# The first half of a mixing product as one block of 1024 columns, three of its eight pairs in seven products instead of eight

## The chip, the cores and the metric

The kernel runs on one core of a Trainium2 chip. Its engines work side by side, each through its own list of instructions in order: TensorE (PE: matmuls, and PEld, the loads of their stationary operand), VectorE (DVE), ScalarE (ACT), GpSimd (POOL) and SyncE (SP, which here only issues DMAs). The metric is the device time of one execution in microseconds; lower is better.

## The reference, cut to what matters

One decoder layer on 256 tokens of 2048 features in float32: a half feed-forward, two token mixers side by side (retention and windowed attention), a second half feed-forward, and a gated embedding, each followed by a layer norm. The change touches the product that joins the two mixers:

```python
mixed = (jax.nn.sigmoid(gate_r) * ret_branch + jax.nn.sigmoid(gate_a) * att_branch) @ w_mix_out[i]
h = layer_norm(alpha * h + mixed, ln_g[i, 1], ln_b[i, 1])
```

The matrix `w_mix_out` is 2048 x 2048.

## The kernel before, in words

**Float32 by three matmuls.** Every float32 operand is split into a high part of a format that PE takes at full speed and a low part, which is the rest (`split`, L97 to L99: ACT writes the high part, then DVE subtracts it from the value to get the low one). One product of 128 x 128 by 128 x 512 then is three matmuls: low by high, high by high, high by low (`Sum.add`, L367 to L376). The order is that: the low part of the tokens' operand is the first thing that PE reads.

**The mixing product before.** Tokens are in two halves t of 128. The 2048 features that are summed over come in 16 groups k of 128, two groups to a *pair* p (0 to 7). The 2048 output columns are made in four blocks of 512 (`mo0` to `mo3`), with one PSUM bank per block and token half; there are eight banks. `tokens_out` (L386) goes through the eight chunks of one block; a chunk is the weights of one pair for 512 columns (128 x 1024 numbers, 512 KB) and costs 2 groups x 2 halves x 3 = 12 matmuls. The residual `y[blk]` is loaded from DRAM when the block starts; after the block DVE adds 1.19 times it (L1474) and takes the statistics of the layer norm (`block_stats`, L744). The fourth block goes through another routine with the norm.

**The features.** The product's left operand is made just before it. The retention block `mr1` ends with DVE forming two arrays of 512 features, `sig[2]` and `sig[3]` (L1454, L1455). PE turns them (transposes, 128 x 128 at a time; `turned`, L1428 to L1436), two groups at a time, and ACT and DVE split the turned values into `mix_t[p]`. Pairs 0 to 3 were turned during `mr1`; pairs 4 to 7 are turned while the first mixing block already runs. These turns are *side jobs*: a list `side`, of which `run_side` (L310) takes one after every chunk or unit of the matmuls. One idle job stands ahead of the four turns. `run_side` also advances `lazy`, which here makes operands for the second feed-forward ahead of time and stores them to DRAM (`sums_ahead`, L219: two DVE sums, a few side steps later two more, then two low parts, and stores on SP's queue).

**Sevens.** In other parts of the kernel (feed-forwards, gates, `mr0` and `mr1`) a block of 1024 columns takes some pairs as *sevens*: a product of 2 x 2 blocks (two token halves, two groups of features; two groups of features, two column halves) with seven block products in place of eight, so 21 matmuls for 24 (`block`, L404). A seven needs more of DVE. Its weights (`Seven.make`, L160) take four sums of weight blocks and four low parts, where the two plain chunks that it replaces take two low parts. On the side of the features it needs four combinations `f5`, `f6`, `f7`, `f3` of the quarters of two groups (`seven_forms`, L438; with `whole`, which puts high and low back together, and a split of the result: `forms_of`, L460, makes those of two pairs at once). Steps go to four extra banks `p1`, `p6`, `p7`, `q5` and to three of the four result banks; after the last seven DVE and ACT combine the extra ones (`seven_common`, L476, the *fold*). In a seven that is not the last, the order of steps is p1 (no form), q2 (no form), q3 (form `f3`), q5, p7, p6, q4; in the last one it is p1, q5 (form `f5`), p6, p7, q2, q3, q4. The retention blocks have sevens for pairs 0 and 1, and their forms (`mrf`) are made well ahead, during the attention's product.

**What sets the order of the work.** All instructions are emitted in a fixed order; an engine never takes a later one first. A planner (`fill`, L260) emits loads and preparations ahead of use. It counts time in matmuls (12 for a plain chunk, 21 for a seven) and space in slots of 128 x 1024 numbers. It prepares the next loaded item while less than 45 of matmul time is ready and the item's `makes` fit (2 slots for a plain chunk, 6 for a seven, which then keeps 7), and loads the next planned one while ready and loaded together stay below 90. `slots_for_weights(16)` sets its room for the mixing product. It is called in `done`, that is, after the matmuls of each chunk or seven have been emitted and before `run_side`. A tile is bound to its place when it is first written; an engine that gets there early waits for the last reader of what was there.

Of the kernel before, what the change touches and what calls it, by code (L numbers as in the profile page):

```python
# [12 lines left out]
ALU = mybir.AluOpType  # L13
PSUM = bass.MemoryType.PSUM

P = 128
S = 256
# [5 lines left out]
ALPHA = 2.0**0.25  # L23
LN_EPS = 1e-5
GN_EPS = 1e-5
KD = D // P
# [29 lines left out]
def layer(ctx: ExitStack, tc: tile.TileContext, io):  # L56
    nc = tc.nc
    sync, act, dve, pool, pe = nc.sync, nc.scalar, nc.vector, nc.gpsimd, nc.tensor
# [8 lines left out]
    def bank(name):  # L67
        return psum.tile([P, 512], F32, tag="ps", name=name)

    def banks(name):  # L70
        return [bank(name + str(j)) for j in range(2)]
# [217 lines left out]
    def take(key):  # L289
        if not ready:  # L290
            fill(True)
        u = ready.pop(0)
        assert u.key == key, (u.key, key)
        return u

    def done(u):
        room["used"] -= u.keeps
        fill()
# [7 lines left out]
    side = []  # L306
    lazy = []
    idle = lambda: None

    def run_side(n=1):  # L310
        for _ in range(n):
            if side:
                side.pop(0)()
        if lazy and next(lazy[0], "end") == "end":
            lazy.pop(0)
# [65 lines left out]
    def tokens_chunk(chunk, k0, lhs, sums, ts, kks=(0, 1)):  # L381
        for kk in kks:
            for t in ts:
                sums[t].add(half_of(lhs(k0 + kk), t), chunk.columns(kk))

    def tokens_out(key, n_k, lhs, ps, n=512, before=None):  # L386

        nk = 1024 // n
        sums = [Sum(ps[t][:, :n], n_k) for t in range(2)]
        for c in range(n_k // nk):  # L390
            u = take(key + (c,))
            tokens_chunk(u.chunk, c * nk, lhs, sums, (0, 1), range(nk))
            done(u)
            run_side()

    def block_units(units, keys):

        for kind, p in units:
            if kind == "P":
                plan.extend(Single(keys(n, p)) for n in range(2))  # L400
            else:
                plan.append((Seven if kind == "S" else Prepared)(keys(0, p), keys(1, p)))

    def block(name, units, keys, lhs, forms, sums, fold, before=None):  # L404


        sevens = [p for kind, p in units if kind != "P"]
        if sevens:
            p1, p6, p7, q5 = (Sum(bank(f"{name}s{j}"), len(sevens)) for j in range(4))
        for j, (kind, p) in enumerate(units):  # L410
            if before is not None:
                before(j)
            if kind == "P":
                for n in range(2):
                    u = take(keys(n, p))
                    tokens_chunk(u.chunk, 2 * p, lhs, [sums[t][n] for t in range(2)], (0, 1))
                    done(u)
                    run_side()
                continue
            u = take(keys(0, p))  # L420
            a11, a12 = (half_of(lhs(2 * p + e), 0) for e in range(2))
            a22 = half_of(lhs(2 * p + 1), 1)
            f5, f6, f7, f3 = forms(p)
            q2, q3, q4 = sums[0][0], sums[0][1], sums[1][0]
            steps = [
                (p1, a11, u.b11), (q2, a12, u.b21), (q3, f3, u.b22), (q5, f5, u.t1),
                (p7, f7, u.t3), (p6, f6, u.t2), (q4, a22, u.t4),
            ]
            if p == sevens[-1]:
                steps = [steps[j] for j in (0, 3, 5, 4, 1, 2, 6)]  # L430
            for to, left, right in steps:
                to.add(left, right)
            done(u)
            run_side()
            if p == sevens[-1]:
                fold(p1.ap, p6.ap, p7.ap, q5.ap)
# [23 lines left out]
    def forms_of(parts, name):  # L460
        hi, lo = (slot([P, 8, P], F32R, name + w) for w in "hl")
        return seven_forms(whole(parts, name + "w"), hi, lo)
# [8 lines left out]
    def block_sums(ps, units, n_k):  # L471

        s = sum(kind == "S" for kind, p in units)
        return [[Sum(ps[t][n], n_k - (2 * s if t and n else s)) for n in range(2)] for t in range(2)]

    def seven_common(p1, p6, p7, q5):  # L476

        e, w = slot([P, 2, 512], F32, "eve"), slot([P, 2, 512], F32, "evw")
        act.copy(e[:, 0], p1)
        dve.tensor_tensor(w[:, 0], e[:, 0], p6, ALU.add)  # L480
        dve.tensor_tensor(e[:, 1], w[:, 0], p7, ALU.add)
        dve.tensor_tensor(w[:, 0], q5, w[:, 0], ALU.subtract)
        dve.tensor_tensor(w[:, 1], q5, e[:, 1], ALU.subtract)
        return e, w
# [257 lines left out]
    def block_stats(stats, y, col):  # L742
        for t in range(2):
            dve.bn_stats(stats[:, t, col, :], y[col][:, t])  # L744

    def load_columns(src, col, name):
        v = slot([P, 2, 512], F32, f"{name}{col}")
        sync.dma_start(v, src[col])
        return v
# [4 lines left out]
    def load_for_norm(i):  # L754

        vectors.append(ln_vectors(i))
        if i < 2:
            p_raws.append(slot([P, 2, S], F32, "praw"))
            sync.dma_start(p_raws[0], io["pT"])
# [320 lines left out]
    GATE_UNITS = units_of("PPSSPSSP", (0, 1, 2, 3))  # L1080
    RET_UNITS = units_of("PPPSPSPP", (0, 1))
    gate_keys = lambda b: lambda n, p: ("w_in_f2", 29 + 4 * b + 2 * n, p)
    ret_keys = lambda b: lambda n, p: ("w_ret2", 4 * b + 2 * n, p)

    def plan_mixers():
        plan_tokens(("w_rv", 0), KD)
        for grp in range(8):
            plan_features([("w_in_f", grp)], KD)
        for blk in range(1, 4):
            plan_tokens(("w_rv", blk), KD)  # L1090
        for grp in range(8, 16, 2):
            plan_tokens(("w_in_f2", grp), KD)
        plan_tokens(("w_av",), KD, nk=4)
        for grp in (20, 16, 17, 18, 19):
            plan_features([("w_in_f", grp)], KD)
        for grp in range(21, 29, 2):
            plan_tokens(("w_in_f2", grp), KD)
        for b in range(2):
            block_units(GATE_UNITS, gate_keys(b))
        for j in range(0, 8, 2):  # L1100
            plan_tokens(("w_att2", j), KD // 2)
        for b in range(2):
            block_units(RET_UNITS, ret_keys(b))
        for blk in range(4):
            plan_tokens(("w_mix", blk), KD)

    def later(n, job):
# [5 lines left out]
    def mixers(ht, norm, residual, keepers, away):  # L1113
# [18 lines left out]
        ps = banks("rv0")  # L1132
# [16 lines left out]
        for grp in range(8):  # L1149
            ps = banks(f"rqk{grp}")  # L1150
# [6 lines left out]
        for blk in range(1, 4):  # L1157
            ps = banks(f"rv{blk}")
# [99 lines left out]
        for h in range(0, HR, 2):  # L1258
            ps = banks(f"rg{h}")
# [16 lines left out]
        ps = banks("av")  # L1276
# [114 lines left out]
        made = {}  # L1391
        forms = lambda p: made[p // 2](p % 2)
        slots_for_weights(18)
        sig = []
        for j in range(4):
# [5 lines left out]
            ps = banks(f"gt{j}")  # L1401
# [3 lines left out]
                act.copy(sig[-1][:, t], ps[t])  # L1405
        assert not side

        def mixer_block(name, units, keys, lhs):

            ps = [banks(name + w) for w in "ab"]  # L1410
            got = []
            block(name, units, keys, lhs, forms, block_sums(ps, units, KD), lambda *a: got.extend(seven_common(*a)))
            for n in range(2):
                for t in range(2):
                    dve.tensor_tensor(got[n][:, t], got[n][:, t], ps[t][n], ALU.add)
            return got
# [5 lines left out]
        mix_t = []  # L1422
        y = {}
# [15 lines left out]
        for j in range(4):  # L1439
            v = sig[4 + j]  # L1440
# [7 lines left out]
        for b in range(2):  # L1448
            for v in sig[2 * b : 2 * b + 2]:
                act.activation(v, v, AF.Sigmoid)  # L1450
            pr = mixer_block(f"mr{b}", RET_UNITS, ret_keys(b), lambda k: of_pairs(ret_t, k))
            for n in range(2):
                j = 2 * b + n
                dve.tensor_tensor(sig[j], sig[j], pr[n], ALU.mult)  # L1454
                dve.tensor_tensor(sig[j], sig[j], sig[4 + j], ALU.add)  # L1455
            side.append(idle)
            side.extend(lambda v=v, kk=kk: turned(v, kk) for v in sig[2 * b : 2 * b + 2] for kk in (0, 2))

        stats = small.tile([P, 2, 4, 6], F32, tag="stats", name="mixst", bufs=1)
# [4 lines left out]
        lhs = lambda k: of_pairs(mix_t, k)  # L1464
        slots_for_weights(16)
        lazy.append(sums_ahead(ahead[8:], 3, 2))
        for blk in range(3):
            if blk == 2:
                load_for_norm(1)
            ps = banks(f"mo{blk}")  # L1470
            y[blk] = load_columns(residual, blk, "mixy")
            tokens_out(("w_mix", blk), KD, lhs, ps)
            for t in range(2):
                dve.scalar_tensor_tensor(y[blk][:, t], y[blk][:, t], ALPHA, ps[t], ALU.mult, ALU.add)  # L1474
            block_stats(stats, y, blk)
        y[3] = load_columns(residual, 3, "mixy")
        ps = banks("mo3")
        sums = [[Sum(ps[t], KD)] for t in range(2)]
# [316 lines left out]
```

## Time and profile before

| | us |
|---|---|
| median of 3 runs | 2271.42 (2270.95 to 2271.64) |
| span of the profiled execution, first to last instruction | 2269.2 |
| PE busy | 2262.1 |
| DVE busy | 1996.8 |
| ACT busy | 1224.6 |
| first mixing matmul, from the span's start | 1379.63 |
| first matmul of the third mixing block | 1425.06 |

The profile gives the span of its execution; its whole time is not shown apart from that. A row of the order of time reads: start, time taken, engine, line, operation, what it writes and reads, shapes, how many in a row, and in brackets how long the engine stood idle before it and what ended that. A matmul's time taken is its latency: 0.39 us, though a new one starts about every 0.23 us. DVE's and ACT's operations overlap a little at the ends too, so starts are compared rather than durations. A row of waits reads: who waited, for whom, in total, how many times, the longest. In names, numbers of buffers are left out: `mo` is any of the mixing blocks' banks, `mixt` the turned features, `lw_mix` and `hw_mix` the low and high parts of its weights, `uw_`/`vw_` a seven's sums, `mrfh`/`mrfl` the parts of the retention's forms.

### The profile page before, as it was taken

What the parts mean: (1) busy time and instruction counts of PE and PEld (TensorE: products, weight loads), DVE (VectorE), ACT (ScalarE), POOL (GpSimd) and SP (SyncE); (2) the same over time, 40 slices, a digit from 0 to 9 for tenths busy, and PEclk for the clock granted to TensorE, in tenths of its full rate; (3) what the DMA queues carried; (4) which work ended last, traced back from release to release, by engine and by line L of the source; (5) the groups of instructions that cost most, each with busy time, mean ns of one, the idle gap of its engine ahead of it and who ended that gap; (6) DMA issues with size and microseconds to landing.
All of it is one profiled execution on the core that took longest, in us unless ns stands there. A gap on an engine that the chain in (4) does not pass through costs nothing.

```text
span 2269.2 us, 29180 instructions
## 1 busy us (share of the span) xinstructions
PE 2262.1 (100%) x10497; PEld 1880.1 (83%) x10497; DVE 1996.8 (88%) x2586; ACT 1224.6 (54%) x1493; POOL 2.3 (0%) x9
## 2 busy tenths in 40 slices
PE   9999999999999999999999999999999999999998
PEld 8888888888888888888778888888888888888887
DVE  7999999999989887888789788689999999889887
ACT  6555555556555444445566554455555565555543
POOL 0000000000000000000000000000000000000000
PEclk9999999999999999999999999999999999999999
DMA  8666665665587878765446668787867766555872
GB/s 301 206 202 195 197 212 177 205 205 187 211 287 258 293 284 295 255 227 190 145 154 219 194 203 294 278 287 241 299 242 250 257 197 218 197 189 210 290 268 75
DMA packets 211130, 515.72 MB, mean 227 GB/s; under 512 B 16413, under 2 KB 20893, under 8 KB 210985
## 3 DMA queue, kind: packets, MB, share of 16 engines
q1 hardware_dynamic: 209000, 511.28, 66.4%
q10 hardware_dynamic: 1984, 2.58, 0.4%
q8 instruction: 82, 1.34, 0.2%
q14 instruction: 64, 0.52, 0.1%
HBM read 484.43 MB, written 29.36 MB: 226 GB/s over the span
## 4 chain that ended last, share of the span: by engine, by line
PE 99%; DVE 0%; ACT 0%; issue 0%; ACTq 0%; POOL 0%; POOLq 0%
PE f1g L376 3%; PE f1g L374 3%; PE f1g L375 3%; PE f2g L376 3%; PE f2g L374 3%; PE f2g L375 3%; PE rqk L325 3%; PE f1u L376 2%; PE f1u L374 2%; PE f1u L375 2%; PE f2u L374 2%; PE f2u L376 2%; PE f2u L375 2%; PE aqk L325 2%; PE f2d L374 2%; PE f1d L375 2%
## 5 line engine op out<-in xcount | busy, mean ns | idle before, releaser
L99 DVE TENSOR_TENSOR lf_gu<-rf_gu,hf_gu 128x1024 fp32r<-128x1024 f32 (+1 forms) x274 | 323.3, 1211 | 13.1 <-ACT hf_gu L98 12.2
L98 ACT CAST hf_gu<-rf_gu 128x1024 fp32r<-128x1024 f32 (+1 forms) x274 | 274.1, 1043 | 29.9 <-DMA rf_gu<-in_f_gu 29.6
L99 DVE TENSOR_TENSOR lf_down<-rf_down,hf_down 128x1024 fp32r<-128x1024 f32 x150 | 178.8, 1220 | 17.4 <-ACT hf_down L98 15.3
L99 DVE TENSOR_TENSOR lw_in_f<-rw_in_f,hw_in_f 128x1024 fp32r<-128x1024 f32 x140 | 167.5, 1219 | 24.9 <-ACT hw_in_f L98 24.7
L98 ACT CAST hf_down<-rf_down 128x1024 fp32r<-128x1024 f32 x150 | 151.8, 1050 | 48.8 <-DMA rf_down<-in_f_down 22.3
L98 ACT CAST huf_gu<-uf_gu 128x1024 fp32r<-128x1024 f32 x70 | 73.8, 1054 | 146.6 <-DVE uf_gu L171 135.1
L98 ACT CAST hw_in_f<-rw_in_f 128x1024 fp32r<-128x1024 f32 x140 | 140.3, 1050 | 3.0 <-PE rv L375 1.4
L374 PE MATMUL f1g<-hf_gu,xt 128*128 128x512 f32 x247 | 96.5, 391 | 0.0
L376 PE MATMUL f1g<-lf_gu,xt 128*128 128x512 f32 x247 | 96.4, 390 | 0.0
L375 PE MATMUL f1g<-hf_gu,xt 128*128 128x512 f32 x247 | 96.1, 389 | 0.0
L98 ACT CAST hvf_gu<-vf_gu 128x1024 fp32r<-128x1024 f32 x70 | 73.8, 1054 | 29.9 <-DVE vf_gu L173 29.2
L971 ACT ACTIVATE eve<-eve 128x1024 f32<-128x1024 f32 x20 | 21.2, 1062 | 126.1 <-DVE eve L970 126.1
L99 DVE TENSOR_TENSOR luf_gu<-uf_gu,huf_gu 128x1024 fp32r<-128x1024 f32 x70 | 85.3, 1219 | 0.0
L99 DVE TENSOR_TENSOR lvf_gu<-vf_gu,hvf_gu 128x1024 fp32r<-128x1024 f32 x70 | 85.3, 1218 | 0.0
L374 PE MATMUL f2g<-hf_gu,ht 128*128 128x512 f32 x217 | 84.6, 390 | 0.0
L376 PE MATMUL f2g<-lf_gu,ht 128*128 128x512 f32 x217 | 84.5, 390 | 0.0
L375 PE MATMUL f2g<-hf_gu,ht 128*128 128x512 f32 x217 | 84.4, 389 | 0.0
L374 PE MATMUL f1u<-hf_gu,xt 128*128 128x512 f32 x212 | 83.4, 393 | 0.0
L376 PE MATMUL f1u<-lf_gu,xt 128*128 128x512 f32 x212 | 82.5, 389 | 0.0
L375 PE MATMUL f1u<-hf_gu,xt 128*128 128x512 f32 x212 | 82.5, 389 | 0.0
L374 PE MATMUL f2u<-hf_gu,ht 128*128 128x512 f32 x172 | 68.2, 397 | 0.0
L376 PE MATMUL f2u<-lf_gu,ht 128*128 128x512 f32 x172 | 66.9, 389 | 0.0
(1465 smaller groups left out, 6558.1 us busy)
## 6 DMA issues: line engine op xcount, KB each, us to landing
rf_gu<-in_f_gu SPq DMA_DIRECT2D x360, 512.0 KB
rf_down<-in_f_down SPq DMA_DIRECT2D x176, 512.0 KB
rw_in_f<-in_w_in_f SPq DMA_DIRECT2D x148, 512.0 KB
rw_rv<-in_w_rv SPq DMA_DIRECT2D x32, 512.0 KB
rw_ret<-in_w_ret SPq DMA_DIRECT2D x32, 512.0 KB
rw_mix<-in_w_mix SPq DMA_DIRECT2D x32, 512.0 KB
rw_pg<-in_w_pg SPq DMA_DIRECT2D x32, 512.0 KB
rw_att<-in_w_att SPq DMA_DIRECT2D x16, 512.0 KB
```

What stands on the lines that cost most here:

```text
L98: act.copy(dst_hi, src)
L99: (lo_engine or dve).tensor_tensor(dst_lo, src, dst_hi, ALU.subtract)
L325: pe.matmul(ps[f], hi[:, kk, f * P : (f + 1) * P], rhs(k), start=k == 0, stop=k == n_k - 1,)
L374: pe.matmul(o, al, bh, start=first, stop=False)
L375: pe.matmul(o, ah, bh, start=False, stop=False)
L376: pe.matmul(o, ah, bl, start=False, stop=self.left == 0)
L971: act.activation(g, g, AF.Silu)
```

## The change

Blocks 0 and 1 of the mixing product become one block of 1024 columns, `mos`, which goes through `mixer_block` and `block` like the retention blocks. Its units in order are plain pairs 0, 1, 2 (two chunks each, named P0n0, P0n1 and so on by column half), sevens of pairs 4 and 5, plain pair 3, the seven of pair 6, plain pair 7. The sevens thus stand on features that are turned last. Their forms are made in `before_mix`, a function that `block` calls ahead of each unit: those of pairs 4 and 5 right ahead of the seven of pair 4, those of pairs 6 and 7 right ahead of the seven of pair 6, where the residuals of both blocks are loaded as well. The features' turns get two idle jobs ahead of them instead of one, so they come after P1n0, P1n1, P2n0 and P2n1. After the block the residual is added in two operations of 1024 in place of four of 512. Blocks 2 and 3 stay as they were. In `block`, the four extra banks are taken when the first seven is reached, not when the block starts; this holds for every block with sevens.

```diff
         sevens = [p for kind, p in units if kind != "P"]
-        if sevens:
-            p1, p6, p7, q5 = (Sum(bank(f"{name}s{j}"), len(sevens)) for j in range(4))
+        four = []
...
             f5, f6, f7, f3 = forms(p)
+            if not four:
+                four.extend(Sum(bank(f"{name}s{i}"), len(sevens)) for i in range(4))
+            p1, p6, p7, q5 = four
...
+    MIX_UNITS = [("P", 0), ("P", 1), ("P", 2), ("S", 4), ("S", 5), ("P", 3), ("S", 6), ("P", 7)]
+    mix_keys = lambda n, p: ("w_mix", n, p)
...
-        for blk in range(4):
+        block_units(MIX_UNITS, mix_keys)
+        for blk in range(2, 4):
             plan_tokens(("w_mix", blk), KD)
...
-        def mixer_block(name, units, keys, lhs):
+        def mixer_block(name, units, keys, lhs, before=None):
...
-            side.append(idle)
+            side.extend((idle,) * (1 + b))
             side.extend(lambda v=v, kk=kk: turned(v, kk) for v in sig[2 * b : 2 * b + 2] for kk in (0, 2))
...
-        for blk in range(3):
-            if blk == 2:
-                load_for_norm(1)
-            ps = banks(f"mo{blk}")
-            y[blk] = load_columns(residual, blk, "mixy")
-            tokens_out(("w_mix", blk), KD, lhs, ps)
-            for t in range(2):
-                dve.scalar_tensor_tensor(y[blk][:, t], y[blk][:, t], ALPHA, ps[t], ALU.mult, ALU.add)
+        def before_mix(j):
+            if j in (3, 6):
+                made[j // 3 + 1] = forms_of(mix_t[4 + (j == 6) * 2 :][:2], f"mof{j}")
+            if j == 6:
+                for blk in range(2):
+                    y[blk] = load_columns(residual, blk, "mixy")
+
+        for blk, v in enumerate(mixer_block("mos", MIX_UNITS, mix_keys, lhs, before_mix)):
+            dve.scalar_tensor_tensor(y[blk], y[blk], ALPHA, v, ALU.mult, ALU.add)
             block_stats(stats, y, blk)
+        load_for_norm(1)
+        ps = banks("mo2")
+        y[2] = load_columns(residual, 2, "mixy")
+        tokens_out(("w_mix", 2), KD, lhs, ps)
+        for t in range(2):
+            dve.scalar_tensor_tensor(y[2][:, t], y[2][:, t], ALPHA, ps[t], ALU.mult, ALU.add)
+        block_stats(stats, y, 2)
```

More of the change, by code (lines that the diff above doesn't have):

```diff
@@ L1406, in mixers @@
         assert not side
-        def mixer_block(name, units, keys, lhs):
+        def mixer_block(name, units, keys, lhs, before=None):
             ps = [banks(name + w) for w in "ab"]
             got = []
-            block(name, units, keys, lhs, forms, block_sums(ps, units, KD), lambda *a: got.extend(seven_common(*a)))
+            block(name, units, keys, lhs, forms, block_sums(ps, units, KD), lambda *a: got.extend(seven_common(*a)), before)
             for n in range(2):
```

## The prediction

> **What bounds the kernel now.** I read the page first, then what TensorE (PE) waits for, then the stretch that the change rewrites, then VectorE (DVE) in order of time.
>
> ```profile
> span 2269.2 us, 29180 instructions
> PE 2262.1 (100%) x10497; PEld 1880.1 (83%) x10497; DVE 1996.8 (88%) x2586; ACT 1224.6 (54%) x1493; POOL 2.3 (0%) x9
> PE 99%; DVE 0%; ACT 0%; issue 0%; ACTq 0%; POOL 0%; POOLq 0%
> PE warm L1674 <- POOL ident masks.py:199: 1.4, 1, 1.4
> PE pln L1568 <- DVE plnst L1566: 0.2, 1, 0.2
> PE plnt L1559 <- DVE plnm L1554: 0.2, 1, 0.2
> ```
>
> The last three lines are all of PE's waits: 1.8 us, none in the middle. So every matmul removed shortens the run by one spacing, and every microsecond that PE is made to wait is added; nothing later can absorb it. The stretch at stake is the first two blocks of the mixing product, from its first matmul (1379.63) to the first of the third block (1425.06).
>
> ```profile
> 1379.63:1425.06 45.43, 45.43 (x210) 37.60 (x208) 38.05 (x42) 23.55 (x26) 0.00 (x0) 1.00 0.83 289
> 1375.78 0.39 PE L375 MATMUL mr1a<-hw_ret,rett 128*128 128x512 f32 x1
> 1379.63 0.39 PE L374 MATMUL mo<-hw_mix,mixt 128*128 128x512 f32 x1
> 1425.06 0.39 PE L374 MATMUL mo<-hw_mix,mixt 128*128 128x512 f32 x1
> 1320.58 0.39 PE L374 MATMUL mr0s<-huw_ret,mrfl 128*128 128x512 f32 x1
> ```
>
> The first row's pairs are length, PE, weight loads, DVE, ACT, POOL; then clock, DMA share, GB/s. DVE works 38.05 of 45.43 us: only 7.4 us are free. From 1375.78 to 1379.63 there are 17 spacings: 0.2265 us per matmul. 192 matmuls take 43.49 us; the other 1.94 us are the four turns of the features (0.485 each).
>
> **The change part by part.** *Matmuls.* Three sevens of 21 replace three times 24: 9 x 0.2265 = 2.04 us less on PE. The loads are the same 32 chunks in number and bytes.
>
> *The late accumulators* (`four`). The same four banks are first written by the same matmuls of the first seven, before and after; no instruction moves. I take nothing. A gain is excluded: if taking them early had held banks up, PE would wait in the blocks with sevens, and the waits above show none. A loss would be a seven's first matmuls waiting for a bank that a turn of features still holds, 1.2 us (its cast and low part, priced below); here that lies inside a longer wait.
>
> *DVE's work.* Its prices are start-to-start times:
>
> ```profile
> 1272.42 1.29 DVE L457 TENSOR_TENSOR mrfw<-rett 128x512 f32<-128x512 f32 x2
> 1276.48 1.22 DVE L99 TENSOR_TENSOR mrfl<-sums,mrfh 128x1024 fp32r<-128x1024 f32 x1 [1.17 <-ACT mrfh L98]
> 1344.01 0.68 DVE L170 TENSOR_TENSOR uw_ret<-rw_ret,rw_ret 128x512 f32<-128x512 f32 x1
> 1350.68 1.28 DVE L99 TENSOR_TENSOR mixt<-mxt,mixt 128x512 fp32r<-128x512 f32 x2
> 1351.88 1.22 DVE L99 TENSOR_TENSOR lw_ret<-rw_ret,hw_ret 128x1024 fp32r<-128x1024 f32 x1
> 1385.23 2.35 DVE L99 TENSOR_TENSOR lw_mix<-rw_mix,hw_mix 128x1024 fp32r<-128x1024 f32 x2
> 1387.50 0.68 DVE L99 TENSOR_TENSOR mixt<-mxt,mixt 128x512 fp32r<-128x512 f32 x1
> 1388.10 1.22 DVE L99 TENSOR_TENSOR lw_mix<-rw_mix,hw_mix 128x1024 fp32r<-128x1024 f32 x1
> 1393.33 0.68 DVE L238 TENSOR_TENSOR uf_gu<-rf_gu,rf_gu 128x512 f32<-128x512 f32 x1
> 1394.53 1.22 DVE L99 TENSOR_TENSOR lw_mix<-rw_mix,hw_mix 128x1024 fp32r<-128x1024 f32 x1
> 1398.02 0.69 DVE L242 TENSOR_TENSOR vf_gu<-rf_gu,uf_gu 128x512 f32<-128x512 f32 x1
> 1399.35 2.35 DVE L99 TENSOR_TENSOR lw_mix<-rw_mix,hw_mix 128x1024 fp32r<-128x1024 f32 x2
> 1385.71 0.59 ACT L98 CAST mixt<-mxt 128x512 fp32r<-128x512 f32 x1 [14.56 <-PE mxt L1435]
> 1386.19 1.06 ACT L98 CAST hw_mix<-rw_mix 128x1024 fp32r<-128x1024 f32 x1
> ```
>
> A seven's eight operations: 1344.01 to 1350.68 = 6.67 us; the two plain chunks it replaces: 1385.23 to 1387.50 = 2.27 (1.14 each). One set of feature sums (`forms_of`, with its wait for ACT's cast): 1272.42 to 1277.70 = 5.28. A low part of turned features: 0.60 (1387.50 to 1388.10). The sums made ahead for the next FFN: 1.20 for the first two (1393.33 to 1394.53), 1.33 for the second two (1398.02 to 1399.35), 1.14 for each low part, as for a plain chunk, whose shape it has. Three sevens add 3 x 4.40 = 13.2 and two sets of forms 10.6: 23.8 us against 7.4 free. So it cannot hide, wherever it stands; what matters is how much of it lies ahead of a matmul that needs it. ACT gets nine more operations (two per seven, one per set of forms, one in the fold) of at most 1.06, with 45.43 - 23.55 = 21.9 us free; it is no bound.
>
> *The order on DVE.* DVE works in order, so I follow the planner (`fill`: 45 units of matmul ready, 90 loaded, 16 slots; a seven needs 6 to be made). At the block's start four plain chunks are ready and two plus the first seven loaded. Then: after units 1 and 2 one plain chunk each; after P1's first chunk the seven of pair 4 (exactly 6 slots free), then features 4 and 5, the first two of the sums ahead, features 6; after P2's last chunk the seven of pair 5 (7 slots free), **then** features 7, the second two sums, and only then the forms that pair 4's seven needs.
>
> DVE's last work for the block before ends at 1385.23 in the row above, and nothing ahead of it changes. From there: 2.27 + 6.67 + 1.20 + 1.20 + 0.60 + 6.67 + 0.60 + 1.33 + 5.28 = 25.82, so the forms are ready at 1411.05. None of it can run sooner by having been idle: the turns it needs leave PE up to 1397.9.
>
> PE: 72 matmuls and four turns from 1379.63 end at 1397.88. Steps one and two of the seven use no forms (6 matmuls, to 1399.24); step three begins with the low part of a form, as the row `mr0s<-huw_ret,mrfl` shows for another seven. **First stall: 1411.05 - 1399.24 = 11.8 us.** Behind it stands all of PE; ACT's casts and SP's loads that wait for slots from PE move along with it, DVE does not.
>
> Then PE: 15 matmuls to 1414.45, pair 5 to 1419.21, P3 to 1424.64, three matmuls of the last seven to 1425.32. It needs its forms (pair 6) at its second step. DVE from 1411.05: two plain chunks 2.27, the third seven 6.67, a low part ahead 1.14, P7's two chunks 2.27, another low part 1.14, forms 5.28 = 18.77, to 1429.82. **Second stall: 4.5 us.** Six steps (4.08) and P7 (5.44) end PE's part at 1439.34, against 1425.06 before: +14.3 = -2.04 + 11.8 + 4.5.
>
> *Edits costed at nothing.* The fold (four operations), the four additions of the banks, and two wide residual updates in place of four narrow: beside the third block, whose first four chunks (10.9 us of matmul) are ready. Without that cover the additions and updates would show: four of 0.69 (half of the 1.37 below) and two twice as wide, 5.5 us.
>
> ```profile
> 1424.58 1.37 DVE L1474 SCALAR_TENSOR_TENSOR mixy<-mixy,mo 128x512 f32<-128x512 f32 x2 [5.32 <-PE mo L376]
> 1446.34 1.37 DVE L1474 SCALAR_TENSOR_TENSOR mixy<-mixy,mo 128x512 f32<-128x512 f32 x2 [8.01 <-PE mo L376]
> SPq L112 <- PE mo L376: 42.7, 15, 9.2
> ```
>
> DVE's 8.01 us idle at the end of the third block also takes what is left over of the sums ahead (3.7 us, three side steps later). The extra idle step ahead of the turns moves no work off PE. The two residual loads go on SP's queue from before the block to before the last seven, behind the stores of the sums; issued near 1425 they are needed at 1440, and 512 KB at the stretch's 289 GB/s take 1.8 us. `load_for_norm` stays ahead of the third block. No POOL work moves.
>
> *Clock.*
>
> ```profile
> 2262.95 0.96 PE L1568 MATMUL pln<-lnrow,plnst 66*128 66x512 f32 x3 [0.21 <-DVE plnst L1566]
> 2264.00:2266.00 2.00, 0.00 (x0) 0.00 (x0) 0.59 (x1) 0.75 (x2) 0.00 (x0) 0.86 0.76 271
> 2266.00:2269.20 3.20, 0.00 (x0) 0.00 (x0) 0.00 (x0) 0.00 (x0) 0.00 (x0) 0.50 0.43 158
> ```
>
> With PE idle at the end, the granted clock falls to 0.50 within some 2 us. So I take it that it falls in an 11.8 us stall too; the matmuls after it run slower for a time that no row shows. Up to 4.5 us of that costs nothing: DVE's chain, which ends at 1429.82, does not depend on it, and the second stall shrinks by as much. [...]
>
> **The rivals.** (1) *One stall.* Pair 5's seven or other work slips behind the forms, or DVE is ahead elsewhere. The forms still wait for features 7, whose turn ends on PE at 1397.88, one step before the seven: cast 0.59, low part 0.60, sums ahead 1.33, forms 5.28, to 1405.7. A stall of 6.4 and none later: +4.4, **2275.8**. For it: only order decides. Against: DVE's total ahead of the second forms, 44.6 us from 1385.23, is the same in any order.
> (2) *All hidden*: the forms are on hand at 1399.24, as in the gate block, where forms made at 1146 are used at 1196 without a wait:
>
> ```profile
> 1146.29 1.23 DVE L99 TENSOR_TENSOR gaf1l<-sums,gaf1h 128x1024 fp32r<-128x1024 f32 x1 [1.17 <-ACT gaf1h L98]
> L374 PE MATMUL ga0s<-huw_in_f,gaf1l x4: 389/389/389, 1196.1 to 1200.9; 128*128 128x512 f32 x4
> ```
>
> Then **2269.4**, just faster. It turns on the forms finishing 11.8 us sooner; here features 7 precedes them in DVE's order.
> (3) *The clock costs besides.* The second stall drops the clock again, and what follows it is slowed. The bounds are 0 and 5.4 us (all 24 matmuls of P7 at the 0.50 of the row above, twice 0.2265 each); I take a third, 1.8, nearer to nothing since the stall is short: **2287.5**. For: the fall above. Against: a stall of 4.5 us or less.
> (4) *Loads or slots late.* SP's loads wait for PE's slots up to 9.2 us (row above); if the last seven's chunks come that late behind the stalled PE, its make slips some 4 us: **2290**. Against: SP ran over ten microseconds ahead of PE here.
>
> **How the numbers follow.** The sum is against the span, 2269.2 to 2283.5; the median of the runs shown, 2271.42, is 2.2 above, so 2285.7. Chances: forecast 0.62, (1) 0.14, (2) 0.07, (3) 0.12, (4) 0.05. The forecast's own range is 2282 to 2289; for 8 in 10 I reach to (1) and (4): 2275.5 to 2291. A measurement tells about 0.2% (4.5 us) from no change. The nine matmuls are all there is to win, 0.09%: faster 0.01. Within: nearly all of (2) and half of (1), whose 4.4 us lie on that border: 0.13. Slower: 0.86.
>
> **What would show it.** In the changed profile: PE waiting on the seven's step with a form of pair 4, released by DVE's low part of the forms, 10 to 13 us long; a second wait of 3 to 5 us at the last seven; DVE without a gap between 1380 and the second forms but for the two waits on ACT; the clock below 1.00 after the first stall; 72 plain matmuls replaced by 63 of sevens. I am wrong if the forms stand ahead of pair 5's seven on DVE, if PE's order puts work between features 7 and the first seven, or if a chunk's load, not DVE, ends PE's wait.

## The result, and the profile after

The changed kernel takes 2290.12 us (median of four runs, 2287.84 to 2291.20) where the kernel before took 2271.53 (four runs, 2270.95 to 2271.95). The ratio is 1.0081, 95% interval 1.0068 to 1.0093: 18.6 us slower. The forecast was 2285.7 us, with a range of 2275.5 to 2291, and slower. The sign and the mechanism came out. The 2290.12 us lie outside the forecast's own range of 2282 to 2289, though, and inside the wider one only because rival (4) had stretched it to 2291 for a reason that did not occur; that much is luck. 4.4 us are missing, and where they are is the subject of most of what follows.

From the page of the changed kernel, its span and its busy times; then PE's longest waits:

```profile
span 2286.0 us, 29212 instructions
PE 2263.7 (99%) x10488; PEld 1881.1 (82%) x10488; DVE 2021.9 (88%) x2624; ACT 1231.8 (54%) x1502; POOL 2.3 (0%) x9
...
PE mosa L374 <- DVE mof3l L99: 11.6, 1, 11.6
PE lnps L625 <- DVE mixy L613: 1.9, 2, 1.4
PE moss L374 <- DVE mof6l L99: 1.7, 1, 1.7
```

Nine matmuls fewer, as counted, and three new waits: two in the rewritten block, on the two sets of forms, and one in the layer norm behind the fourth block. The order of time on DVE and PE in the rewritten block, the row of its whole stretch (length, PE, weight loads, DVE, ACT, POOL, then clock, DMA share, GB/s) and the start of the second feed-forward:

```profile
1379.75 0.39 PE L374 MATMUL mosa<-hw_mix,mixt 128*128 128x512 f32 x1
1409.86 1.23 DVE L99 TENSOR_TENSOR mof3l<-sums,mof3h 128x1024 fp32r<-128x1024 f32 x1 [1.11 <-ACT mof3h L98]
1411.14 0.79 PE L374 MATMUL mosa<-bw_mix,mof3l 128*128 128x512 f32 x1 [11.64 <-DVE mof3l L99]
1428.59 1.23 DVE L99 TENSOR_TENSOR mof6l<-sums,mof6h 128x1024 fp32r<-128x1024 f32 x1 [1.17 <-ACT mof6h L98]
1429.87 0.50 PE L374 MATMUL moss<-huw_mix,mof6l 128*128 128x512 f32 x1 [1.72 <-DVE mof6l L99]
1439.52 0.39 PE L374 MATMUL mo<-hw_mix,mixt 128*128 128x512 f32 x1
1379.75:1439.52 59.77, 46.41 (x200) 37.55 (x199) 56.84 (x73) 26.41 (x30) 0.00 (x0) 0.89 0.60 210
1491.78 0.39 PE L374 MATMUL f2g<-hf_gu,ht 128*128 128x512 f32 x1
```

The block takes 59.77 us for 45.43, 14.34 more. DVE is busy in 56.84 of them and PE in 46.41: for the length of this block DVE has become the bound. Between the first mixing matmul and the end of the second forms its only waits are the two for ACT in the rows above, 1.11 and 1.17 us. The kernel before started its second feed-forward here:

```profile
1475.13 0.39 PE L374 MATMUL f2g<-hf_gu,ht 128*128 128x512 f32 x1
```

I therefore cut each run in three: the block (first mixing matmul to the first matmul of the third block), the norm part (from there to the first `f2g` matmul), and the rest to the end of the span.

| us | block | norm part | rest | sum of the differences |
|---|---|---|---|---|
| kernel before | 45.43 | 50.07 | 794.07 | |
| changed kernel | 59.77 | 52.26 | 794.22 | +14.34 +2.19 +0.15 = 16.7 |

The remaining 0.1 of the spans' difference of 16.8 lies ahead of the block. The profiled execution (2287.84) was the quickest of the four runs; against their medians 1.8 us more are to be explained.

### The profile page after: what moved, and what is told of

It reads as the page before. It is cut to its first block, busy times and chain, and to the rows that moved or that the text cites. A ratio compares the mean times of both kernels' runs of the same rounds, so it can differ in the third digit from the quotient of the medians.

```text
span 2286.0 us, 29212 instructions
## 1 busy us (share of the span) xinstructions
PE 2263.7 (99%) x10488; PEld 1881.1 (82%) x10488; DVE 2021.9 (88%) x2624; ACT 1231.8 (54%) x1502; POOL 2.3 (0%) x9
## 4 chain that ended last, share of the span: by engine, by line
PE 97%; DVE 2%; ACT 0%; DMA 0%; issue 0%; ACTq 0%; POOL 0%; SPq 0%; DVEq 0%; POOLq 0%
PE f1g L374 3%; PE f1g L375 3%; PE f1g L376 3%; PE f2g L376 3%; PE f2g L375 3%; PE f2g L374 3%; PE rqk L325 3%; PE f1u L376 2%; PE f1u L374 2%; PE f1u L375 2%; PE f2u L374 2%; PE f2u L375 2%; PE f2u L376 2%; PE aqk L325 2%; PE f2d L376 2%; PE f1d L376 1%
## 5 line engine op out<-in xcount | busy, mean ns | idle before, releaser
L99 DVE TENSOR_TENSOR lf_gu<-rf_gu,hf_gu 128x1024 fp32r<-128x1024 f32 (+1 forms) x274 | 323.5, 1212 | 15.1 <-ACT hf_gu L98 13.7
```

What stands on the lines that cost most here:

```text
L99: (lo_engine or dve).tensor_tensor(dst_lo, src, dst_hi, ALU.subtract)
```

## The experiments

My theory at the start: DVE's total work ahead of a matmul sets when that matmul can run, in whatever order the work stands, and the falling clock costs nothing since DVE's chain ends the block. The rivals: the order is at fault, the clock is, or the late banks are.

**The late banks alone.** In the kernel before:

```diff
-        if sevens:
-            p1, p6, p7, q5 = (Sum(bank(...)) for j in range(4))
+        four = []
...
+            if not four:
+                four.extend(Sum(bank(...)) for i in range(4))
```

> The kernel before with one part of the change alone: the four extra banks are taken at a block's first seven. My reason (the same banks are first written by the same matmuls, so nothing moves): 2271.5 us, within 0.1% of the kernel before, and no wait of PE that the kernel before did not have. Rival (the late banks carry part of the 18.6 us): 2274 or more, with PE waiting in the blocks with sevens.

2271.37 us against 2271.42, ratio 1.0000 (0.9991 to 1.0009), and no wait that the kernel before lacks. This part of the change does nothing.

**The first forms one unit earlier.**

```diff
-            if j in (3, 6):
-                made[j // 3 + 1] = forms_of(...)
+            if j in (2, 6):
+                made[2 + (j == 6)] = forms_of(...)
```

> The changed kernel with the forms of pairs 4 and 5 made one unit earlier on DVE, ahead of unit P2 and so ahead of pair 5's seven. My theory (DVE's total ahead of the second set of forms decides, and that total is the same in any order): the first stall shrinks from 11.6 to some 3 us, but PE waits again for the weights of pair 5 or P3, the second forms still end at 1429.8, and the third block still begins at 1439.5 (within 1 us); the time stays within 3 us of the changed kernel. Rival (only the place of the forms in DVE's order is at fault): the first stall goes and nothing takes its place; 9 us less, about 2281.

2291.25 us, 1.0087 of the kernel before (1.0073 to 1.0100). Its PE rows with waits, its third block, and its clock in two-microsecond windows (the third number from the end of each row):

```profile
1402.30 0.50 PE L374 MATMUL mosa<-bw_mix,mof2l 128*128 128x512 f32 x1 [2.45 <-DVE mof2l L99]
1410.16 0.79 PE L374 MATMUL moss<-hvw_mix,mof2l 128*128 128x512 f32 x1 [5.50 <-DVE mixt L99]
1430.22 0.80 PE L374 MATMUL moss<-huw_mix,mof6l 128*128 128x512 f32 x1 [5.48 <-DVE mof6l L99]
1442.13 0.39 PE L374 MATMUL mo<-hw_mix,mixt 128*128 128x512 f32 x1
...
1406.00:1408.00 2.00, 0.00 (x0) 0.00 (x0) 2.00 (x3) 2.00 (x4) 0.00 (x0) 0.93 0.86 332
1414.00:1416.00 2.00, 2.00 (x9) 1.57 (x9) 1.93 (x4) 1.00 (x1) 0.00 (x0) 0.86 0.03 11
1428.00:1430.00 2.00, 0.00 (x0) 0.00 (x0) 1.06 (x1) 2.00 (x3) 0.00 (x0) 0.55 1.06 420
1434.00:1436.00 2.00, 2.00 (x9) 1.56 (x8) 1.50 (x3) 0.27 (x1) 0.00 (x0) 0.74 1.03 422
```

The first wait shrinks from 11.64 to 2.45, and 5.50 and 5.48 appear behind it: 13.43 us in all, for 13.36 in the changed kernel. The wait of 5.50 is not for the weights of pair 5 or P3, as I expected, but for a bank: the matmul's weights and form were ready by 1402.3, and the bank that it is the first of its seven to write was still held by the last turn of features, whose low part (`mixt`) stands behind pair 5's seven on DVE here. In both kernels the wait for the second forms ends 50.1 us after the first mixing matmul. That total work counts and not order stands, and the rival that saw 9 us to win falls. But the third block begins 62.02 us after this run's first mixing matmul (1380.11), not 59.8: the clock fell a second time, in the last wait, and the matmuls behind it ran at a granted clock of 0.50 until 1435.0. I had not expected that here.

**The first stall filled with matmuls.** 51 extra matmuls into a bank that is overwritten later:

```diff
+            for at, (to, left, right) in enumerate(steps):
+                if name == "mos" and p == sevens[0] and at == 2:
+                    for _ in range(51):
+                        pe.matmul(q5.ap, a11[0], u.b11[0], start=True, stop=True)
```

> The changed kernel with 51 more matmuls (11.6 us at 0.2265 each) into a bank that is overwritten later, ahead of the first matmul that needs the forms of pair 4: extra work that fills the first stall and changes no output. My theory (DVE's chain ends the block, and the slower clock only takes what the second stall would have been): the granted clock stays at 1.00 through the block, the second stall grows from 1.7 to 4.4 us, the third block still begins at 1439.5, and the time is that of the changed kernel within 1 us. Rival (the fall of the clock costs by itself): the second stall does not grow, the third block begins 2 to 2.8 us sooner, and the time is as much less.

2291.00 us, 1.0085 (1.0071 to 1.0099). PE's only wait in the block, the third block, and the clock:

```profile
1430.40 0.63 PE L374 MATMUL moss<-huw_mix,mof6l 128*128 128x512 f32 x1 [4.13 <-DVE mof6l L99]
1441.66 0.39 PE L374 MATMUL mo<-hw_mix,mixt 128*128 128x512 f32 x1
...
1410.00:1430.00 20.00, 16.19 (x71) 12.72 (x69) 18.23 (x22) 10.65 (x13) 0.00 (x0) 1.00 0.93 318
1430.00:1432.00 2.00, 1.59 (x4) 1.30 (x5) 2.00 (x3) 2.00 (x4) 0.00 (x0) 0.66 1.03 324
1434.00:1436.00 2.00, 2.00 (x11) 1.63 (x10) 1.61 (x3) 0.72 (x1) 0.00 (x0) 0.99 1.04 424
```

With the clock at 1.00 up to the second wait, that wait grew from 1.72 to 4.13, as the theory had it; the rival's 2 to 2.8 us were not there to win. But around a wait of 4.13 us the clock fell too (at 1430.64, 0.24 us after the wait's end), for 3.4 us, and behind the forms it counts: the block took 61.38 us (from 1380.28), 1.6 more than with the fall in the first stall. So the theory was half right: the fall in the first stall costs nothing *because* it shortens the second wait to 1.72 us, and there the clock stayed at 1.00.

**The sums ahead made later.** They leave the mixing product:

```diff
-        lazy.append(sums_ahead(ahead[8:], 3, 2))
...
         norm.run(steps, lhs, ((8, (0, 0)), (10, (0, 1)), (10, "sums")), (2, 3))
+        lazy.append(sums_ahead(ahead[8:], 3, 2))
```

> The changed kernel with the sums that are made ahead for the second feed-forward left out of the mixing product and made in that feed-forward, behind the norm. My theory (DVE's work decides): 1.20 + 1.33 = 2.53 us go from ahead of the first forms, 2 x 1.14 = 2.28 more from ahead of the second, so the first stall is 9.1 us, the second forms end at 1425.0 and the third block begins at 1434.7, 4.8 us sooner than in the changed kernel at most (4.5 if the clock falls as long). If the 2.4 us that the norm behind the fourth block lost come from SP's loads queued behind the stores of these sums, they are gone too: 2283; if they come from the places of the tiles, they stay: 2285.6. Rival (DVE's order matters, not its total): the second stall is no smaller, and the third block begins at 1437 or later.

2286.20 us, 1.0064 (1.0052 to 1.0077). PE's two waits in it, and its third block:

```profile
1408.47 0.79 PE L374 MATMUL mosa<-bw_mix,mof3l 128*128 128x512 f32 x1 [9.19 <-DVE mof3l L99]
1434.52 0.39 PE L374 MATMUL mo<-hw_mix,mixt 128*128 128x512 f32 x1
1589.93 0.75 PE L374 MATMUL f22s<-huf_gu,f2fl 128*128 128x512 f32 x1 [3.22 <-ACT f2a L918]
```

The block took 54.99 us (from 1379.53), 4.78 less than the changed kernel's for 4.81 us of DVE work taken out, with one stall of 9.19 and no second one. The norm part took 49.93: its loss went as well. The total missed 2283 because the work came back where it was put: PE waits 3.22 us for ACT in the second feed-forward, and the rest of the run is 799.35 for 794.07. Whether that is the price of the move itself, the same move in the kernel before shows.

> The kernel before with the sums ahead moved out of the mixing product into the second feed-forward, as in the run with the changed kernel; the first blocks of the mixing product stay plain. In that run the time from the first matmul of the second feed-forward to the end was 5.3 us longer than before, with a wait of 3.2 us of PE for ACT. If that is the price of making the sums later, it is paid here too: 2276 to 2277. Rival (that loss is something that the changed mixing product pushed ahead of itself): 2271.5, no wait.

2276.40 us against 2270.99, 1.0023 (1.0014 to 1.0033), with this wait:

```profile
1580.97 0.80 PE L374 MATMUL f22s<-huf_gu,f2fl 128*128 128x512 f32 x1 [3.27 <-ACT f2a L916]
```

It is: 5.4 us. Of the two places the mixing product is the cheaper one for the sums, and the sevens take the room that they use there.

**The stores of the sums on another queue.** For the 2.19 us of the norm part. First SP's wait for a low part of these sums, between 1440 and 1470 in the changed kernel; then the rows of SP's queue (start, time issuing, what is moved), and ACT's, DVE's and PE's rows behind them:

```profile
SPq L252 <- DVE luf_gu L248: 5.2, 1, 5.2
1451.45 0.33 SPq L252 DMA_DIRECT2D ludf_gu<-luf_gu  x1
1454.86 0.33 SPq L255 DMA_DIRECT2D lvdf_gu<-lvf_gu  x1
1461.29 0.81 SPq L112 DMA_DIRECT2D rw_pp<-in_w_pp  x2
1467.79 1.05 ACT L98 CAST hw_pp<-rw_pp 128x1024 fp32r<-128x1024 f32 x1 [1.59 <-DMA rw_pp<-in_w_pp]
1481.16 0.68 DVE L1467 SCALAR_TENSOR_TENSOR mixy<-mixy,mo 128x512 f32<-128x512 f32 x1
1484.60 0.44 PE L625 MATMUL lnps<-ident,mixy 128*128 128x128 f32 x2 [1.40 <-DVE mixy L613]
```

The same store and load in the kernel before:

```profile
1430.57 0.33 SPq L255 DMA_DIRECT2D lvdf_gu<-lvf_gu  x1
1439.56 0.85 SPq L112 DMA_DIRECT2D rw_pp<-in_w_pp  x2
```

The last store of a low part leaves 24.3 us later than it did, the load of `w_pp` 21.7 later, where the third block is 14.5 later. Two readings were open: the loads stand behind these stores, or DVE itself is late. One edit tells them apart:

```diff
-                sync.dma_start(away[e], parts[e].bitcast(F32))
+                (queue or sync).dma_start(away[e], parts[e].bitcast(F32))
...
-        lazy.append(sums_ahead(ahead[8:], 3, 2))
+        lazy.append(sums_ahead(ahead[8:], 3, 2, pool))
```

> The changed kernel with the stores of the sums ahead on POOL's queue instead of SP's; everything on PE, DVE and ACT stays in its order. The block with sevens must end as in the changed kernel (third block at 1439.5 to 1441.7). Theory 1 for the 2.2 to 2.4 us lost between the third block and the second feed-forward (SP's loads stand behind stores that wait for DVE's late low parts): the loads come some 5 us sooner, PE's two waits in the norm are gone, 2.2 us less than the changed kernel. Theory 2 (DVE itself is that far behind, and the places of the tiles that it has yet to read hold the loads up): no more than 0.5 us less.

2285.63 us, 1.0064 (1.0051 to 1.0077); the changed kernel, run beside it, took 2288.42, 1.0076 (1.0062 to 1.0089). The rows that answer to those:

```profile
1455.75 1.21 SPq L112 DMA_DIRECT2D rw_pp<-in_w_pp  x1
1464.62 1.06 ACT L98 CAST hw_pp<-rw_pp 128x1024 fp32r<-128x1024 f32 x1 [3.11 <-DMA rw_pp<-in_w_pp]
1478.06 0.69 DVE L1467 SCALAR_TENSOR_TENSOR mixy<-mixy,mo 128x512 f32<-128x512 f32 x1 [0.22 <-PE mo L376]
1489.72 0.39 PE L374 MATMUL f2g<-hf_gu,ht 128*128 128x512 f32 x1
```

All else stands in its order. The block is unchanged (59.78), and DVE is no sooner: its last low part of the sums is stored at 1455.38 here. But the first load of `w_pp` leaves 5.5 us sooner (the second only 0.1), and ACT's casts of the two come 3.2 and 2.5 us sooner. The norm's first operation on DVE stands behind all the low parts `lf_gu`. In the changed kernel the last two of those had waited 1.09 and 1.11 us for ACT's casts; here none waits, and the operation itself waits for PE. The norm part takes 49.93 us, 0.14 less than before the change. The first reading holds: stores that wait for DVE held up the loads behind them on SP.

> The changed kernel once more, for the 2.3 us by which most of its runs are longer than the profiled one. If they lie in the clock (the low phase falls otherwise, the second stall is longer, and the clock falls again in it): the third block begins near 1441.5, with less than 1.00 of the clock behind the second forms, and PE's second wait is 3 to 4.5 us. If they lie in the norm: the third block begins at 1439.5 and PE waits there for 3 to 4 us.

```profile
1439.53 0.39 PE L374 MATMUL mo<-hw_mix,mixt 128*128 128x512 f32 x1
1485.56 0.44 PE L625 MATMUL lnps<-ident,mixy 128*128 128x128 f32 x2 [2.35 <-DVE mixy L613]
```

In this second profile of the changed kernel the block is the same to 0.02 us, and the norm part is 0.94 longer. So what differs between these two executions is the norm part. The clock fell at almost the same time in both (1402.7 and 1402.9), so they do not show what it would do if it fell at another. The three longer runs of the result (2290.0 to 2291.2) have no trace; that their time lies in the norm too is likely, and not shown.

**Forms for the pair that needs them.** The second set is made for pairs 6 and 7; no seven reads pair 7's.

```diff
-            if j in (3, 6):
-                made[j // 3 + 1] = forms_of(mix_t[4 + (j == 6) * 2 :][:2], f"mof{j}")
+            if j == 3:
+                made[2] = forms_of(mix_t[4:6], "mof3")
+            if j == 6:
+                made[3] = forms_of_one(mix_t[6], "mof6")
```

> The changed kernel with the second set of forms made for pair 6 alone; the changed kernel makes them for pair 7 as well, which no seven reads. DVE's set gets half as wide: from 5.28 to some 2.9 us, so the second forms end at 1427.4. Theory (DVE's chain decides): the second stall goes (PE is there at 1427 to 1428 after the slow clock), the third block begins at 1437.3 to 1437.7, 2 us sooner than in the changed kernel's profile, or 4 us sooner where the clock fell there a second time; 2286 to 2288. Rival (something else releases the last seven): the third block begins at 1439.5 or later and the time stays at 2290.

2286.95 us, 1.0068 (1.0056 to 1.0081).

```profile
1427.75 0.50 PE L374 MATMUL moss<-huw_mix,mof6l 128*128 128x512 f32 x1 [0.39 <-DVE mof6l L99]
1437.41 0.39 PE L374 MATMUL mo<-hw_mix,mixt 128*128 128x512 f32 x1
```

The block is 2.08 us shorter (57.69), as DVE's prices say. The time came down by 1.5 only: PE reached the norm sooner and waited there longer (norm part 53.66 for 53.20 in the changed kernel beside it).

> The changed kernel with two of the edits together: the second forms for pair 6 alone, and the stores of the sums on POOL's queue. If the loss in the norm comes from SP's order and the other from DVE's chain, they add: 2.1 and 2.9 us less than the changed kernel in the same runs (2288.4), 2283.4. If the norm's loss is only moved by the one (PE comes 2 us sooner and waits 2 us longer, as with the forms of pair 6 alone) and not by the other: 2285.6, no better than the stores alone.

2283.97 us, 1.0055 (1.0042 to 1.0069); block 57.72, norm part 50.43. The two gains, 1.5 and 2.8, make 4.3, and together they gave 4.45 against the same runs of the changed kernel (2288.42): they add.

**One seven, two sevens.** Fewer sevens, on pairs whose features are turned before the block, placed late. First the one, then what the two have in its place:

```diff
-    MIX_UNITS = [..., ("S", 4), ("S", 5), ("P", 3), ("S", 6), ("P", 7)]
+    MIX_UNITS = [..., ("P", 4), ("P", 5), ("P", 6), ("S", 3), ("P", 7)]
...
-            side.extend((idle,) * (1 + b))
+            side.append(idle)
...
+            if j == 4:
+                made["mix"] = forms_of_one(mix_t[3], "mof4")
```

```diff
+    MIX_UNITS = [("P", 0), ("P", 1), ("P", 4), ("P", 5), ("P", 6), ("S", 2), ("S", 3), ("P", 7)]
...
+            if j == 4:
+                made[1] = forms_of(mix_t[2:4], "mof4")
```

> The block of 1024 columns with one seven instead of three: pair 3, whose features are turned before the block, as the last unit but one; its forms are made for that pair alone, the idle job ahead of the turns is gone. DVE gets 4.40 us for the seven and some 3 for its forms, 7.4 in all, just what it has free in these two blocks. In order on DVE: in the kernel before, the low parts of the eighth chunk end at 1401.6; then sums ahead 1.14, forms 3.1, the seven 6.67, to 1412.5; PE comes to the seven at 1379.63 + 1.94 + 144 x 0.2265 = 1414.2. My theory (DVE's total work ahead of a matmul decides): no stall, PE saves 3 x 0.2265 = 0.68 us, the third block begins at 1424.4; 2270.3 against 2271.0, within what can be measured. Rival (a block of this form costs in itself, by its fold, its wide updates or its loads): 2272.5 or more, with a wait of PE.

> The same with two sevens, pairs 2 and 3, both turned early, one behind the other ahead of the last pair, forms of both in one set. DVE gets 8.80 + 5.28 = 14.1 us, 6.7 more than it has free. In order: low parts of the sixth chunk at 1398.0 (kernel before), sums 1.33, the first seven 6.67, sums 1.14, forms 5.28, to 1412.4; PE is there after 1379.63 + 1.94 + 126 x 0.2265 = 1410.1: a first stall of 2.3. The second seven 6.67 to 1419.1 against PE at some 1416: 1 to 1.5 more. With 6 x 0.2265 = 1.36 us less of matmuls the third block begins at 1427 to 1428, 2 to 3 us later than in the kernel before; 2273 to 2276 (its norm may lose too). Rival (only sevens on features that are turned late cost time): no stall, 2269.6.

One seven: 2273.22 us against 2271.28, 1.0010 (1.0001 to 1.0019). Two: 2277.85, 1.0029 (1.0018 to 1.0040). First the rows of the one seven, then those of the two:

```profile
1379.12 0.39 PE L374 MATMUL mosa<-hw_mix,mixt 128*128 128x512 f32 x1
1423.86 0.39 PE L374 MATMUL mo<-hw_mix,mixt 128*128 128x512 f32 x1
1468.58 0.44 PE L639 MATMUL lnps<-ident,mixy 128*128 128x128 f32 x2 [1.03 <-DVE mixy L627]
```

```profile
1412.56 0.50 PE L374 MATMUL mosa<-bw_mix,mof4l 128*128 128x512 f32 x1 [2.15 <-DVE mof4l L99]
1427.91 0.39 PE L374 MATMUL mo<-hw_mix,mixt 128*128 128x512 f32 x1
1440.91 0.50 PE L376 MATMUL mo<-lw_mix,mixt 128*128 128x512 f32 x1 [1.50 <-DVE lw_mix L99]
1413.50:1414.00 0.50, 0.50 (x3) 0.38 (x2) 0.40 (x2) 0.20 (x1) 0.00 (x0) 0.54 1.03 418
```

In the block both came out: with one seven no wait and 44.74 us, 0.69 less than the kernel before; with two a stall of 2.15 (2.3 expected) and 48.13 us from 1379.78, 2.70 more. The wait that I expected at the second seven did not appear; the clock fell behind the first wait (0.54 in the last row) and stayed low for 3.4 us, in which eight matmuls took 3.38 us for 1.81 at 0.2265 each, so PE came to the second seven later. In its place PE waits 1.50 in the third block, for a plain chunk's low part. So DVE's free 7.4 us pay for one seven and not for two, and that the features are turned early does not help. Outside the block I missed in both: the norm part grew to 51.86 and 53.96. By its time, and by a wait of PE, the one seven came out as its rival had it (2272.5 or more); but the wait is in the norm and not in the block. As its DVE work all fits, the stores on SP were the suspect once more. The two sevens' norm was not taken apart further.

> The block with one seven (pair 3, turned early) and the stores of the sums ahead on POOL's queue. The run with one seven alone began its third block 0.69 us sooner, counted from its first mixing matmul, and lost 1.8 us between there and the second feed-forward in its profile (2.0 in the medians). If that loss has the cause that the stores had in the changed kernel (SP's order), it goes with them: 0.7 us less than the kernel before, 2270.5 against some 2271.2, with no wait of PE in the norm. If it comes from DVE's longer work in the third block (fold, four additions), it stays: 2272 to 2273.

2270.41 us (11 runs, 2269.94 to 2271.28) against 2271.12 (15 runs); ratio 0.9997 (0.9988 to 1.0006).

```profile
1424.62 0.39 PE L374 MATMUL mo<-hw_mix,mixt 128*128 128x512 f32 x1
1474.55 0.39 PE L374 MATMUL f2g<-hf_gu,ht 128*128 128x512 f32 x1
```

Block 44.75 us (from 1379.87), norm part 49.93, no new wait: with SP freed of those stores, the saving of the seven's three matmuls is kept. Not every load came sooner. Counted from the third block's first matmul, the first of `w_pp` left 0.7 us later than with the one seven alone, and the first of `f_gu`, the second feed-forward's weights, 2.7 us sooner. The medians differ by 0.71 us, as worked out, but the interval contains 1: this is the best of the versions run, and not shown to be faster than the kernel before.

## Why the prediction was right, and where it was not

*Matmuls.* Nine fewer, 10497 to 10488.

*The order on DVE and the first stall.* Right, item by item in the order forecast. Forms at 1411.05 forecast, 1409.86 + 1.23 = 1411.09 found; the stall 11.8 forecast, 11.64 found.

*The second stall.* The time at which DVE's chain ends was right (1429.82; 1428.59 + 1.23 in the trace). That it agrees to the hundredth is luck: the block itself began 0.12 us later than in the kernel before. The stall was 1.72 for 4.5, and the clock took the rest: PE came to it 2.7 us later than in the sum, counted from the block's start. Forecast was that a loss by the clock behind the first stall would come off the second, with the sum the same; the third block began at 1439.52, for 1439.34. Of the low phase 5.3 us lay behind the restart (1411.14 to 1416.4, below): its twelve matmuls started some 0.43 us apart at a granted clock of 0.50, for 0.2265 at 1.00, which cost 2.6 us. What this rests on, that the clock stays up in the second wait, was in rival (3) and not in the forecast's sum, which had a second stall of 4.5 us and no cost behind it. In the run with the filled stall that wait was 4.13 us, the clock fell, and it cost 1.6 us.

*The late accumulators.* Costed at nothing; alone they do nothing. The loss that I named for them, a seven's matmul waiting for a bank that a turn still holds, came up only with the early forms, and there it was 5.50 us and not 1.2: I had priced the turn's cast and low part, and not the seven that stands ahead of that low part on DVE.

*Edits costed at nothing.* This is the step that failed. I wrote that DVE's 8.01 us idle at the end of the third block takes what is left over of the sums ahead. It does, and DVE still idles 2.57 us there:

```profile
1460.80 1.37 DVE L1487 SCALAR_TENSOR_TENSOR mixy<-mixy,mo 128x512 f32<-128x512 f32 x2 [2.57 <-PE mo L376]
```

But each of those sums ends in stores on SP's queue, and I followed only DVE's half of the step. A store that waits for DVE until 1451 held the loads behind it, and PE waited in the norm. The term was forecast at 0. It measured 2.19 us in the profile, and taking the stores off SP gave 2.8 back in the medians.

*From the span to the median.* I added the 2.2 us of the runs before. The changed kernel's median lies 4.1 above its profiled span, so 1.9 of the 4.4 missing us are here. In the second profile the norm part is 0.94 us longer, so this is probably in part the same failed step; the runs behind the median have no trace.

*DVE's work.* All of it was counted, but I took all of it to be needed. Pair 7's half of the second forms, 2.08 us of the block, is read by nothing. A count of who reads each result would have shown it in the code.

*The rivals.* (1) one stall, and (2) all hidden: against them DVE's total, which the run with early forms bore out. (3) the clock costs besides: not in the changed kernel, but its mechanism is real: the block is 1.6 us longer with the filled stall and 2.3 with the early forms. (4) loads late, 2290: its number was the one measured, its place was not. The last seven's chunks were in time; the loads that came late were those of the norm, 20 us later, and their queue was held by DVE's stores and not by PE's slots.

## What to carry to other kernels

Where an engine works in order and is nearly full, count all its work ahead of each operand, and don't look for a better order until that total fits: here 7.4 free us paid for one seven (4.40 and 3.1 us of DVE), and three sevens made two stalls. When a step is made later, follow its stores as well: on a queue that also carries loads, a store that waits holds the loads behind it (here SP waited 5.2 us for one low part), and the wait shows up stages later. And ask of each prepared operand who reads it.

## What of the hardware I had not expected

In the three runs below, each stretch in which the granted clock was 0.50 lasted about 3.4 us, or two or four times as long. Their ends are read from the clock in the windows above, as a mean of 1.00 and 0.50: 1430.64 to 1434.04 in the run with the filled stall (3.4), 1407.7 to 1414.6 and 1428.2 to 1435.0 with the early forms (6.8 each), and in the changed kernel four times 3.4:

```profile
1402.00:1404.00 2.00, 0.00 (x0) 0.00 (x0) 2.00 (x3) 0.53 (x1) 0.00 (x0) 0.68 0.14 57
1416.00:1418.00 2.00, 2.00 (x9) 1.64 (x8) 2.00 (x4) 1.90 (x2) 0.00 (x0) 0.90 0.78 255
```

A 0.68 is 36% of the window at 1.00, so the clock fell at 1402.7; a 0.90 is 20% at 0.50, so it came back at 1416.4: 13.7 us.

Nor had I expected which of the shorter waits are followed by a fall. With two sevens a wait of 2.15 us, alone, was followed by one at 1413.5, 0.9 us after its end. A wait of 2.45 with the early forms was not: the nine matmuls behind it took 2.36 us in all, and the clock fell at 1407.7, in the next wait. Nor was one of 1.72 in the changed kernel, where the clock is 1.00 in every two-microsecond window from 1424 to 1440. So of waits of about two microseconds one cost the clock and two did not, and the longest of the three was not the one that did: by these three, the length of a wait alone does not tell.
